# RMS statistics in the MLP phases: eight TensorE sums replaced by a VectorE reduction and two TensorE sums

## The chip, the cores and the metric

The kernel runs on all 8 cores of one Trainium2 chip (trn2). Each core does one half of one sequence, with no communication. The time of an execution is the device time of the slowest core, in microseconds (us). The kernel before takes 1516.05 us in the median of its first three runs (1514.5, 1516.05 and 1701.93). The run of 1701.93 us is counted as slow, a state that some executions had: the cores of one die (cores 0 to 3 or 4 to 7) show a lower granted clock and take longer.

## The reference, cut to what matters

A two-layer backbone block over 4096 tokens of 1024 channels. Every sub-layer starts with an RMS norm, and so does the output:

```python
def rmsnorm(x, g):
    xf = x.astype(jnp.float32)
    y = xf * lax.rsqrt(jnp.mean(xf * xf, axis=-1, keepdims=True) + EPS)
    return (y * g.astype(jnp.float32)).astype(x.dtype)

def sq_relu_mlp(h, w1, w2):
    return jnp.square(jax.nn.relu(h @ w1)) @ w2
# per layer: x = x + g1 * mixer(modulate(rmsnorm(x))); x = x + g2 * sq_relu_mlp(modulate(rmsnorm(x)))
```

The mean of squares over the 1024 channels of each token is the "statistic" of this document.

## The kernel before

Channels lie on the 128 partitions in eight chunks, tokens along the free dimension. A statistic over N tokens therefore sums over eight chunks and over partitions. ScalarE writes the squares as bf16 `[128, 8, N]`; TensorE multiplies each chunk by a matrix of ones/1024 and sums all eight in one bank of PSUM (here the program's `ps`, eight banks of 512 f32 columns, where its matmuls write), which gives the mean on every partition at once:

```python
def norm_sq(tile, sq, part=0, parts=1):          # ScalarE: squares, in `parts` pieces
    c0, c1 = part * NCH // parts, (part + 1) * NCH // parts
    ...
        P.act(sq[:, c0:c1, o:o + n], xv[:, c0:c1, :], AF.Square)

def norm_stat(sq, N, rs):                        # TensorE: eight matmuls of N columns
    bk = P.bank()
    for c in range(NCH):
        P.mm(bk[:, 0:N], ONESM, sq[:, c, 0:N], start=(c == 0), stop=(c == NCH - 1))
    rms_of(bk, N, rs)                            # ScalarE: Ln, Exp -> 1/rms
```

These pieces are issued among the matmuls of the MLP before, one piece per output group, so that the next norm is done when it is needed. `mlp_1` is the up-projection (eight matmuls per output group, then ScalarE's relu from PSUM into one of two buffers `TMP`, then VectorE's square into the hidden tile); `mlp_2` is the down-projection.

```python
nB = sum([st_norm(gb, i) for i in range(3)], [])
spread(mlp_2(ga), nB, 0)                                         # statistics 1, 2, 3
n4, n0 = l1_norm(4, RS[0]), l1_norm(0, RS[1])                    # 4, 5: issued during mlp_2(gb)
...
spread(mlp_2(l1[0]), st_norm(l1[1], 0) + st_norm(l1[1], 1))      # 6, 7
spread(mlp_1(l1[1]), fin_pieces(0) + fin_pieces(1), 2, 2)        # 8, 9: final norm, first two tiles
```

The order of instructions on each engine isn't written by hand. A list scheduler simulates the engines with a cost per instruction, and fixes the order in which each engine will run its instructions.

```python
def ew_cost(self, eng, kind, out, ins):          # the scheduler's idea of a VectorE duration, in ns
    ...
    if sb and (kind == "one" or b16):
        return 155.0 + 0.6 * n
    return 160.0 + 1.04 * n

def pick(e):                                     # the next instruction of engine e
    lim = head[e] + self.WINDOW[e]
    ...                                          # among those within the window: the one that can start
                                                 # first by the simulated times, older ones preferred
```

On the chip each engine gets its list in that order.

The softmax here doesn't subtract the row's maximum and nothing guards it: scores larger than these inputs give would overflow.

Of the kernel before, what the change touches and what calls it, by code (L numbers as in the profile page):

```python
# [7 lines left out]
BF16 = mybir.dt.bfloat16  # L8
AF = mybir.ActivationFunctionType
ALU = mybir.AluOpType  # L10
# [3 lines left out]
NCH = 8  # L14
# [12 lines left out]


class _Op:
    __slots__ = ("id", "eng", "chan", "fn", "deps", "signal", "waits", "pos", "inc", "sigval", "cost", "mode", "unit", "prio")  # L30


class Sched:
# [7 lines left out]
    def __init__(self, nc):  # L41
        self.nc = nc
        self.ops = []
        self.streams = {k: [] for k in ("pe", "act", "dve", "pool", "sp")}
        self.chan_ops = {}
        self.buckets = {}
        self.base = {}
        self.hold, self.boost = None, 0

    def rects(self, ap):  # L50
        name = ap.tensor.name
# [63 lines left out]

    def op(self, eng, fn, reads=(), writes=(), chan=None, inc=1, extra_deps=(), cost=100.0, mode=None, join=False):
        o = _Op()
        o.cost, o.mode, o.prio = cost, mode, self.boost
        if self.hold is not None and eng == "pe":
            join = self.hold > 0  # L120
            self.hold += 1
        o.unit = join
        o.id = len(self.ops)
        o.eng = eng
        o.chan = chan or eng
        o.fn = fn
        o.inc = inc
        o.signal = chan is not None
        o.waits = []
        o.sigval = 0  # L130
        accs = []
        for ap in reads:
            if ap is None or isinstance(ap, (int, float)):
                continue
            sp, rs = self.rects(ap)
            for r in rs:
                accs.append((sp, r, sp == "ps"))
        for ap in writes:
            sp, rs = self.rects(ap)
            for r in rs:  # L140
                accs.append((sp, r, True))
        o.deps = self._query_insert(o, accs)
        for d in extra_deps:
            o.deps[d.id] = True
        self.ops.append(o)
        self.streams[eng].append(o)
        lst = self.chan_ops.setdefault(o.chan, [])
        lst.append(o)
        o.pos = len(lst)
        return o  # L150
# [22 lines left out]
    def reorder(self):  # L173
        ops = self.ops
        units = {e: [] for e in self.streams}
# [18 lines left out]
        head = {e: 0 for e in units}  # L194
# [3 lines left out]
        dma_free, mode = 0.0, None  # L198
# [11 lines left out]
            return v  # L210

        def pick(e):
            lim = head[e] + self.WINDOW[e]
            cand = []
            for i, v in avail[e].items():
                if i < lim:
                    s = max(free[e], v)
                    if e == "pe" and mode is not None and units[e][i][0].mode != mode:
                        s += 100.0
                    cand.append((s, i))  # L220
            if not cand:
                return None
            lo, li = min(cand)
            tol = lo + min(1500.0, max(150.0, 0.5 * sum(o.cost for o in units[e][li])))
            s, i = min(((s, i) for s, i in cand if s <= tol), key=lambda c: c[1] - units[e][c[1]][0].prio)
            return (s, i)
# [5 lines left out]
        while left:  # L232
            e, b = None, None
            for k in units:
                if best[k] is None and avail[k]:
                    best[k] = pick(k)
                if best[k] is not None and (b is None or best[k][0] < b[0]):
                    e, b = k, best[k]
            s, i = b
            t = s  # L240
            for o in units[e][i]:
                for d in o.deps:
                    if unit_of[d] != (e, i):
                        t = max(t, end[d] + (0.0 if ops[d].chan == e == "pe" else self.SEM))
# [8 lines left out]
            if e == "pe":  # L253
                mode = units[e][i][-1].mode
# [80 lines left out]
class Prog:  # L335
# [87 lines left out]
    def stt(self, out, in0, scalar, in1, op0, op1):  # L423
        return self.S.op("dve", lambda e: e.scalar_tensor_tensor(out, in0, scalar, in1, op0, op1),  # L424
                         reads=[in0, in1, scalar], writes=[out], cost=self.ew_cost("dve", "stt", out, [in0, in1]))

    def shuf(self, out, in_, mask):
        return self.S.op("dve", lambda e: e.stream_shuffle(out, in_, mask), reads=[in_], writes=[out],  # L428
                         cost=190.0 + 1.05 * self.n_of(out))
# [61 lines left out]
def build():  # L491
    nc = bass.Bass("TRN2", target_bir_lowering=False)
    P = Prog(nc)
# [27 lines left out]
    def const(name, shape, dt):  # L521
        off = co[0]
        co[0] += (int(np.prod(shape)) * ESZ[dt] + 31) // 32 * 32
        assert co[0] <= 6144, (name, co[0])
        return P.t(name, off, shape, dt)
# [9 lines left out]
    ONESM = const("onesm", [128], BF16)  # L535
# [5 lines left out]
    IDENT = const("ident", [128], F32)  # L541
    MSK = const("msk", [2, 128], BF16)
    EDGE = const("edge", [8, 8], F32)

    XM = P.t("xm", 6144, [NCH, NM], F32)
    E0 = 71680
# [3 lines left out]
    def ft(name, off, shape, dt):  # L550
        return P.t(name, F0 + off, shape, dt)
# [10 lines left out]
    RSALL = ft("rs", 105472, [1216], F32)  # L562
    RS = [RSALL[:, i * 512:(i + 1) * 512] for i in range(2)]
    TMP = [ft("tmp", 110336 + i * 2048, [512], F32) for i in range(2)]


    MBS = [P.bk(7), P.bk(6)]
# [84 lines left out]
    tiles = [[(XM[:, :, t * 512:(t + 1) * 512], 512, 0)] for t in range(4)]  # L652
# [6 lines left out]
    def sqv(buf, N):  # L659
        return buf[:, 0:NCH * N].rearrange("p (a b) -> p a b", a=NCH)  # L660

    def norm_sq(tile, sq, part=0, parts=1):
        c0, c1 = part * NCH // parts, (part + 1) * NCH // parts
        o = 0
        for xv, n, _ in tile:
            P.act(sq[:, c0:c1, o:o + n], xv[:, c0:c1, :], AF.Square)
            o += n
# [2 lines left out]
        P.act(rs[:, 0:N], bk[:, 0:N], AF.Ln, bias=EPSV)  # L670
        P.act(rs[:, 0:N], rs[:, 0:N], AF.Exp, scale=-0.5)

    def norm_stat(sq, N, rs):
        bk = P.bank()
        for c in range(NCH):
            P.mm(bk[:, 0:N], ONESM, sq[:, c, 0:N], start=(c == 0), stop=(c == NCH - 1))
        rms_of(bk, N, rs)

    def norm_apply(tile, rs, l, n, h, c, eng="act", tmps=None):
# [9 lines left out]
                P.ts(h[:, c, o:o + N], tmp, a, b, ALU.mult, ALU.add, eng=eng)  # L689
            o += N  # L690

    def norm_pieces(tile, h, rs, l, n, eng="act", parts=1, tmps=None):

        N = width(tile)
        return [(lambda i=i: norm_sq(tile, h, i, parts)) for i in range(parts)] + [lambda: norm_stat(h, N, rs)] + \
               [(lambda c=c: norm_apply(tile, rs, l, n, h, c, eng, tmps)) for c in range(NCH)]


# [285 lines left out]
    def mlp_2(st):  # L984
        l, g = st["l"], st["g"]
        for fo in range(NCH):
            bks = [P.bank() for _ in st["pieces"]]
            for hf in range(2):
                w = w_take(("w2", l, g, 2 * fo + hf)).rearrange("p (a b) -> p a b", a=16)
                for ti, tile in enumerate(st["pieces"]):  # L990
                    N = width(tile)
                    bk = bks[ti]
                    for h in range(16):
                        P.mm(bk[:, 0:N], w[:, h, :], st["HID"](ti, 16 * hf + h), start=(hf == 0 and h == 0), stop=(hf == 1 and h == 15))
                    if hf == 1:
                        o = 0
                        for xv, n, col in tile:
                            P.stt(xv[:, fo, :], bk[:, o:o + n], MOD[:, l, 40 + fo, col:col + 1], xv[:, fo, :], ALU.mult, ALU.add)
                            o += n
                    if ti == len(st["pieces"]) - 1:  # L1000
                        ST.free()
                    yield 16 * N * MMN

    def spread(main, side, start=0, every=1):

        side = list(side)
        for i, _ in enumerate(main):
            if i >= start and (i - start) % every == 0 and side:
                side.pop(0)()
        for f in side:  # L1010
            f()
# [15 lines left out]
            st["tmp"] = [ft("tmp", 69120 + i * 1664, [416], F32) for i in range(2)]  # L1027
        return st

    def st_norm(st, ti, eng="act", parts=2):  # L1030
        return norm_pieces(st["pieces"][ti], st["H2"][ti], st["rs"][ti], st["l"], 1, eng, parts, st.get("tmp"))

    ga = l0_state(0, [tiles[4], cols(0, 416), cols(416, 416)])
    gb = l0_state(1, [cols(832, 408), cols(1240, 404), cols(1644, 404)])
# [5 lines left out]
    interleave(out_mm(3), nA[2][2:3] + aA[4:] + aB)  # L1040
    ST.fetch(5)
    run_all(mlp_1(ga))
    nB = sum([st_norm(gb, i) for i in range(3)], [])
    spread(mlp_2(ga), nB, 0)
    run_all(mlp_1(gb))

# [16 lines left out]
    HH = {4: sqv(ft("h", 47104, [NCH * 384], BF16), 384), 0: sqv(HB[0], 512), 1: sqv(HB[1], 512), 2: sqv(HB[0], 512), 3: sqv(HB[1], 512)}  # L1063
# [4 lines left out]
    def wo_c(c):  # L1068
        return WO0 if c == 0 else WO17[:, c - 1, :]

    def l1_norm(t, rs, eng="act", parts=2):
        return norm_pieces(tiles[t], HH[t], rs, 1, 0, eng, parts)

    wq, rope_slots, rope_of = [], [], {}

# [138 lines left out]
            yield 4 * 512 * MMN  # L1214


    n4, n0 = l1_norm(4, RS[0]), l1_norm(0, RS[1])

    def early_dma():
        P.dma("pool", WKV0.rearrange("p a b c -> p (a b c)"), d_wkv, slot="wkv")  # L1220
# [60 lines left out]
    l1 = []  # L1281
# [84 lines left out]
    def fin_pieces(t):  # L1366
        xv = tiles[t][0][0]
        rs = RS[t % 2]

        def fin(c):  # L1370
            P.stt(xv[:, c, :], xv[:, c, :], GVEC[:, 4, c:c + 1], rs, ALU.mult, ALU.mult)
            if c % 2 == 1:
                outs.append(P.dma("sp", d_out[:, c - 1:c + 1, t * 512:(t + 1) * 512], xv[:, c - 1:c + 1, :]))
        return [(lambda i=i: norm_sq(tiles[t], sqv(SQF, 512), i, 4)) for i in range(4)] + \
               [lambda: norm_stat(sqv(SQF, 512), 512, rs)] + [(lambda c=c: fin(c)) for c in range(NCH)]

    run_all(mlp_a)
    spread(mlp_2(l1[0]), st_norm(l1[1], 0) + st_norm(l1[1], 1))
    spread(mlp_1(l1[1]), fin_pieces(0) + fin_pieces(1), 2, 2)
    run_all(mlp_2(l1[1]))  # L1380
    for t in (2, 3):
# [121 lines left out]
```

## Time and profile before

| | before |
|---|---|
| time, median of 3 runs | 1516.05 us |
| TensorE (PE) busy | 1431.5 us, 95% |
| VectorE (DVE) / ScalarE (ACT) / GpSimd (POOL) busy | 40% / 39% / 20% |
| share of the chain that ended last | PE 90% |

The page's first part (busy time of each engine, share of the span, instructions) and its fourth (the chain of work that ended last, by engine) for the kernel before:

```profile
PE 1431.5 (95%) x8436; PEld 694.0 (46%) x8436; DVE 600.9 (40%) x1003; ACT 583.2 (39%) x841; POOL 304.5 (20%) x371
PE 90%; DMA 3%; DVE 2%; issue 2%; ACT 1%; POOL 1%; SPq 0%; DVEq 0%; ACTq 0%; POOLq 0%
```

The table by stretches for the kernel before, in the stretches that hold statistics 1, 5, 6, 8 and 9. The columns are the stretch, its length, then busy us and instruction count of PE, PEld, DVE, ACT and POOL, the granted TensorE clock (1.00 is full), the DMA share and GB/s:

```profile
350.00:400.00 50.00, 50.00 (x316) 27.82 (x315) 12.30 (x25) 18.57 (x24) 4.75 (x9) 1.00 0.59 104
650.00:700.00 50.00, 50.00 (x331) 28.25 (x329) 7.07 (x17) 10.21 (x15) 7.05 (x13) 1.00 0.60 105
1150.00:1200.00 50.00, 50.00 (x233) 22.63 (x232) 12.48 (x18) 18.56 (x20) 3.70 (x7) 1.00 0.44 74
1250.00:1300.00 50.00, 50.00 (x234) 22.66 (x232) 16.21 (x24) 15.06 (x22) 3.70 (x7) 1.00 0.45 77
1300.00:1350.00 50.00, 50.00 (x233) 22.64 (x232) 25.97 (x39) 18.14 (x31) 3.70 (x7) 1.00 0.63 124
```

TensorE has no gap in any of them and runs at full clock. The timeline of TensorE before, at the eighth statistic (start, duration, engine, line, operation, output and inputs, count):

```profile
1287.85 1.89 PE L387 MATMUL ps<-h_135,ring_57 128*128 128x512 bf16 x8
1289.58 1.89 PE L387 MATMUL ps<-sqf_176,onesm_46 128*128 128x512 bf16 x8
1291.31 1.89 PE L387 MATMUL ps<-h_136,ring_57 128*128 128x512 bf16 x8
```

From start to start, eight matmuls of 512 columns take 1291.31 - 1289.58 = 1.73 us (216 ns each), whether they do useful products or only sum squares. The printed 1.89 us includes the end of the last, which overlaps the next.

### The profile page before, as it was taken

The page shows a single profiled execution, that of the slowest core. Times are in us where ns is not written, and L with a number is a line of the kernel's source. Part 1 is how long each engine was busy: PE and PEld are TensorE (multiplying, and loading weights), DVE is VectorE, ACT ScalarE, POOL GpSimd, SP SyncE. Part 2 cuts the span into 40 slices and gives each one's busy share as a digit, 9 for nine tenths or more (in the row PEclk, how much of TensorE's full clock was granted, in tenths as well). Part 3 has the DMA queues.
Part 4 walks back from the last instruction along what each step waited for, and adds up shares of the span by engine and source line. Part 5 has one row for each costly group of instructions (what it writes and reads, how often), then busy time and mean ns, then how long its engine had stood idle before and what let it go on. Part 6 is the DMA issues. An engine that isn't in the chain of part 4 may idle for free.

```text
span 1514.3 us, 23295 instructions; the slowest of 8 cores (1505.0 to 1514.3 us)
## 1 busy us (share of the span) xinstructions
PE 1431.5 (95%) x8436; PEld 694.0 (46%) x8436; DVE 600.9 (40%) x1003; ACT 583.2 (39%) x841; POOL 304.5 (20%) x371
## 2 busy tenths in 40 slices
PE   1699999999999999999997999899999999999996
PEld 0344445555555555555543334334444444444442
DVE  0177874443221344322248666443443222552003
ACT  2464363335110333323018778774334121432002
POOL 2025400010100010110135666552000000000000
PEclk9999999999999999999998999999999999999998
DMA  9554715545663455664354000400444444663432
GB/s 193 152 126 70 131 28 94 98 84 90 118 113 63 77 89 104 104 108 74 62 94 74 8 2 2 70 2 15 72 82 70 80 74 71 134 130 70 84 56 111
DMA packets 39808, 124.16 MB, mean 82 GB/s; under 512 B 4240, under 2 KB 4624, under 8 KB 39312
## 3 DMA queue, kind: packets, MB, share of 16 engines
q0 software_dynamic: 29504, 102.90, 39.9%
q1 hardware_dynamic: 10192, 19.76, 4.1%
q8 instruction: 70, 1.15, 0.3%
q14 instruction: 42, 0.34, 0.1%
HBM read 217.15 MB, written 8.39 MB: 149 GB/s over the span
## 4 chain that ended last, share of the span: by engine, by line
PE 90%; DMA 3%; DVE 2%; issue 2%; ACT 1%; POOL 1%; SPq 0%; DVEq 0%; ACTq 0%; POOLq 0%
PE ps L387 89%; DMA xm_55<-xT 2%; DMA ring_59<-ada_r 1%; DVE xm_55 L424 0%; SPq L447 0%; DVE tmp_65 L414 0%; ACT xb_68 L397 0%; POOL qt_122 L414 0%; ACT rs_63 L397 0%; DVE tb_129 L414 0%; DVE tb_130 L428 0%; DVE tb_127 L414 0%; POOL dt_75 L414 0%; DVE tb_128 L414 0%; DVE tb_130 L414 0%
## 5 line engine op out<-in xcount | busy, mean ns | idle before, releaser
L424 DVE SCALAR_TENSOR_TENSOR xm_55<-ps,mod_44,xm_55 128x512 f32<-128x512 f32 (+2 forms) x136 | 97.4, 718 | 296.4 <-PE ps L387 296.1
L397 ACT ACTIVATE tmp_64<-ps 128x512 f32<-128x512 f32 (+2 forms) x156 | 84.8, 543 | 213.6 <-PE ps L387 161.8
L397 ACT ACTIVATE tmp_65<-ps 128x512 f32<-128x512 f32 (+2 forms) x157 | 85.3, 544 | 159.5 <-PE ps L387 98.1
L397 ACT ACTIVATE sqf_176<-xm_55 128x1024 bf16<-128x1024 f32 x16 | 16.7, 1053 | 158.9 <-DVE xm_55 L424 156.9
L387 PE MATMUL ps<-xb_68,win_67 128*128 128x512 bf16 (+1 forms) x192 | 50.2, 422 | 10.2 <-ACT xb_68 L397 9.5
L387 PE MATMUL ps<-h_0_98,ring_61 128*128 128x408 bf16 (+3 forms) x336 | 58.9, 335 | 0.0
L387 PE MATMUL ps<-h_0_98,ring_58 128*128 128x384 bf16 (+3 forms) x336 | 58.9, 335 | 0.0
L414 DVE TENSOR_TENSOR tmp_64<-xm_55,rs_63 128x512 f32<-128x512 f32 (+2 forms) x44 | 33.8, 767 | 48.2 <-ACT rs_63 L397 41.9
L397 ACT ACTIVATE rs_63<-ps,epsv_51 128x512 f32<-128x512 f32 (+3 forms) x16 | 10.6, 666 | 105.2 <-PE ps L387 104.9
L387 PE MATMUL ps<-hid_99,ring_61 128*128 128x416 bf16 (+3 forms) x288 | 51.0, 335 | 0.0
L387 PE MATMUL ps<-h_0_98,ring_60 128*128 128x416 bf16 (+3 forms) x288 | 50.5, 335 | 0.0
L387 PE MATMUL ps<-h_0_98,ring_57 128*128 128x416 bf16 (+3 forms) x288 | 50.4, 335 | 0.0
L387 PE MATMUL ps<-h_0_98,ring_59 128*128 128x416 bf16 (+3 forms) x288 | 50.4, 335 | 0.0
L447 POOL DMA_DIRECT2D ring_59<-w_r x27 | 14.3, 531 | 171.8 <-PE ps L387 171.7
L414 DVE TENSOR_TENSOR hid_100<-tmp_64 128x416 bf16<-128x416 f32 (+3 forms) x48 | 27.9, 581 | 43.8 <-ACT tmp_64 L397 43.8
L414 DVE TENSOR_TENSOR hid_99<-tmp_64 128x416 bf16<-128x416 f32 (+3 forms) x48 | 27.9, 581 | 41.2 <-ACT tmp_64 L397 41.1
L387 PEld LDWEIGHTS ps<-h_0_98,ring_61 128*128 128x128 bf16 x336 | 32.5, 97 | 25.1 <-issue 0.6
L387 PEld LDWEIGHTS ps<-h_0_98,ring_58 128*128 128x128 bf16 x336 | 32.4, 98 | 25.0 <-issue 0.8
L447 POOL DMA_DIRECT2D ring_61<-w_r x27 | 14.3, 530 | 143.3 <-PE ps L387 143.1
L414 DVE TENSOR_TENSOR hid_99<-tmp_65 128x416 bf16<-128x416 f32 (+3 forms) x48 | 27.9, 581 | 37.7 <-ACT tmp_65 L397 37.7
L414 DVE TENSOR_TENSOR hid_100<-tmp_65 128x416 bf16<-128x416 f32 (+3 forms) x48 | 27.9, 581 | 36.0 <-ACT tmp_65 L397 36.0
L447 POOL DMA_DIRECT2D ring_60<-w_r x24 | 12.7, 530 | 138.4 <-PE ps L387 103.7
(803 smaller groups left out, 3136.9 us busy)
## 6 DMA issues: line engine op xcount, KB each, us to landing
ring_61<-w_r POOLq DMA_DIRECT2D x27, 512.0 KB, 5.7
ring_59<-w_r POOLq DMA_DIRECT2D x27, 512.0 KB, 5.8
ring_58<-w_r POOLq DMA_DIRECT2D x26, 512.0 KB, 5.8
ring_57<-w_r POOLq DMA_DIRECT2D x24, 512.0 KB, 5.8
ring_60<-w_r POOLq DMA_DIRECT2D x24, 512.0 KB, 5.9
outT<-xm_55 SPq DMA_DIRECT2D x16, 512.0 KB, 4.9
xm_55<-xT SPq DMA_DIRECT2D x6, 1024.0 KB, 9.0
ring_58<-ada_r POOLq DMA_DIRECT2D x12, 512.0 KB, 5.2
```

The source lines that it names most:

```text
L387: return self.S.op("pe", lambda e: e.matmul(out, lhsT, rhs, start=start, stop=stop), reads=[lhsT, rhs], writes=[out], cost=max(30.0 if hal ...
L397: return self.S.op("act", lambda e: e.activation(out, in_, func, bias=bias, scale=scale), reads=[in_, scale, bias], writes=[out], cost=175 ...
L414: return self.S.op(eng, lambda e: e.tensor_tensor(out, in0, in1, op), reads=[in0, in1], writes=[out], cost=self.ew_cost(eng, "tt", out, [i ...
L424: return self.S.op("dve", lambda e: e.scalar_tensor_tensor(out, in0, scalar, in1, op0, op1), reads=[in0, in1, scalar], writes=[out], cost= ...
L447: return self.S.op(q, lambda e: e.dma_start(out=out, in_=in_), reads=[in_], writes=[out], chan="dma:" + slot, inc=16, extra_deps=dep, cost ...
```

## The change

The sum over the eight chunks moves to VectorE, which has time; only one vector of sums per partition is left for TensorE. That vector is f32, and to keep its precision in bf16 matmuls it is split in two bf16 parts (the rounded value and the rest), so two matmuls remain of eight. Only the nine statistics listed above are changed. The core of the diff:

```diff
+    def addc(self, out, in_):
+
+        return self.S.op("dve", lambda e: e.tensor_reduce(out, in_.rearrange("p c n -> p n c"), mybir.AxisListType.X, ALU.add),
+                         reads=[in_], writes=[out], cost=160.0 + 1.04 * self.n_of(in_))
...
+    SQHI = const("sqhi", [512], BF16)
...
     TMP = [ft("tmp", 110336 + i * 2048, [512], F32) for i in range(2)]
+    SQLO = ft("sqlo", 110336 + 2048, [512], BF16)
...
-    def norm_stat(sq, N, rs):
+    def norm_stat(sq, N, rs, red=False):
         bk = P.bank()
-        for c in range(NCH):
-            P.mm(bk[:, 0:N], ONESM, sq[:, c, 0:N], start=(c == 0), stop=(c == NCH - 1))
+        if red:
+            P.addc(TMP[0][:, 0:N], sq[:, :, 0:N])
+            P.copy(SQHI[:, 0:N], TMP[0][:, 0:N])
+            P.tt(SQLO[:, 0:N], TMP[0][:, 0:N], SQHI[:, 0:N], ALU.subtract)
+            P.mm(bk[:, 0:N], ONESM, SQHI[:, 0:N], start=True, stop=False)
+            P.mm(bk[:, 0:N], ONESM, SQLO[:, 0:N], start=False, stop=True)
+        else:
+            for c in range(NCH):
+                P.mm(bk[:, 0:N], ONESM, sq[:, c, 0:N], start=(c == 0), stop=(c == NCH - 1))
         rms_of(bk, N, rs)
...
-    nB = sum([st_norm(gb, i) for i in range(3)], [])
+    nB = sum([st_norm(gb, i, red=True) for i in range(3)], [])
...
-    n4, n0 = l1_norm(4, RS[0]), l1_norm(0, RS[1])
+    n4, n0 = l1_norm(4, RS[0], red=True), l1_norm(0, RS[1], red=True)
...
-               [lambda: norm_stat(sqv(SQF, 512), 512, rs)] + [(lambda c=c: fin(c)) for c in range(NCH)]
+               [lambda: norm_stat(sqv(SQF, 512), 512, rs, t < 2)] + [(lambda c=c: fin(c)) for c in range(NCH)]
...
-    spread(mlp_2(l1[0]), st_norm(l1[1], 0) + st_norm(l1[1], 1))
+    spread(mlp_2(l1[0]), st_norm(l1[1], 0, red=True) + st_norm(l1[1], 1, red=True))
```

(The diff also adds a field `pin` to the scheduler, which nothing sets; it changes no order. The rest passes `red` through.) The reduction reads its input as `p n c`: for each token the eight values lie N bf16 values apart.

More of the change, by code (lines that the diff above doesn't have):

```diff
@@ L29 @@
 class _Op:
-    __slots__ = ("id", "eng", "chan", "fn", "deps", "signal", "waits", "pos", "inc", "sigval", "cost", "mode", "unit", "prio")
+    __slots__ = ("id", "eng", "chan", "fn", "deps", "signal", "waits", "pos", "inc", "sigval", "cost", "mode", "unit", "prio", "pin")
 class Sched:
@@ L47, in __init__ @@
         self.base = {}
-        self.hold, self.boost = None, 0
+        self.hold, self.boost, self.pin = None, 0, False
     def rects(self, ap):
@@ L117, in op @@
         o = _Op()
-        o.cost, o.mode, o.prio = cost, mode, self.boost
+        o.cost, o.mode, o.prio, o.pin = cost, mode, self.boost, self.pin and eng == "pe"
         if self.hold is not None and eng == "pe":
@@ L212, in pick @@
         def pick(e):
-            lim = head[e] + self.WINDOW[e]
+            lim = head[e] + (1 if head[e] < len(units[e]) and units[e][head[e]][0].pin else self.WINDOW[e])
             cand = []
@@ L690, in norm_apply, with norm_pieces @@
             o += N
-    def norm_pieces(tile, h, rs, l, n, eng="act", parts=1, tmps=None):
+    def norm_pieces(tile, h, rs, l, n, eng="act", parts=1, tmps=None, red=False):
         N = width(tile)
-        return [(lambda i=i: norm_sq(tile, h, i, parts)) for i in range(parts)] + [lambda: norm_stat(h, N, rs)] + \
+        return [(lambda i=i: norm_sq(tile, h, i, parts)) for i in range(parts)] + [lambda: norm_stat(h, N, rs, red)] + \
                [(lambda c=c: norm_apply(tile, rs, l, n, h, c, eng, tmps)) for c in range(NCH)]
@@ L1028, in l0_state, with st_norm @@
         return st
-    def st_norm(st, ti, eng="act", parts=2):
-        return norm_pieces(st["pieces"][ti], st["H2"][ti], st["rs"][ti], st["l"], 1, eng, parts, st.get("tmp"))
+    def st_norm(st, ti, eng="act", parts=2, red=False):
+        return norm_pieces(st["pieces"][ti], st["H2"][ti], st["rs"][ti], st["l"], 1, eng, parts, st.get("tmp"), red)
     ga = l0_state(0, [tiles[4], cols(0, 416), cols(416, 416)])
@@ L1069, in wo_c, with l1_norm @@
         return WO0 if c == 0 else WO17[:, c - 1, :]
-    def l1_norm(t, rs, eng="act", parts=2):
-        return norm_pieces(tiles[t], HH[t], rs, 1, 0, eng, parts)
+    def l1_norm(t, rs, eng="act", parts=2, red=False):
+        return norm_pieces(tiles[t], HH[t], rs, 1, 0, eng, parts, red=red)
     wq, rope_slots, rope_of = [], [], {}
```

## The prediction

> **What bounds the kernel now.** TensorE. The page gives PE 1431.5 us of 1514.3 us (95%); the chain that ended last is 90% PE. In a table by 50 us stretches, PE is busy 50.0 us at a granted clock of 1.00 in every stretch from 200 to 750 us and from 1050 to 1450 us. All nine changed statistics lie there: three in the first layer's MLP down-projection (at 365, 398, 431 us), two in the next one (641, 697), two in the third (1167, 1207), two under the last up-projection (1290, 1336). A TensorE microsecond saved there is a microsecond of the kernel. VectorE (40%) has room.
>
> **Removed.** Of eight matmuls against the ones matrix, two remain. Spacing of starts in the timeline: 216 ns at 512 columns, 171 ns at 404, about 163 ns at 384. Five statistics have 512 columns, three 404 to 408, one 384: 6 x (5 x 0.216 + 3 x 0.171 + 0.163) = 10.5 us, 0.7%.
>
> **Added.** On VectorE, per statistic: a reduction over 8 x N bf16 values, a copy to bf16, a subtraction. No reduction is in the trace. [...]the trace's [...]operation (128x512 f32 product, 0.69 us) gives about 1.04 ns per element plus 0.16 us, so I estimate 4.4 us for 512 columns, 3.5 for 404, 3.4 for 384; copy about 0.45, subtraction 0.58 to 0.69 us. Together about 45 us more VectorE time, off the critical path.
>
> **Moved.** In the instruction order the pairs stand on TensorE exactly where the eight stood, except the last two, which come four output groups (6.9 us) later. The attention stage is unchanged on every engine.
>
> **Does TensorE wait for the chain?** From the end of the last square to the old statistic's start the trace has 6.1 us (first), 6.0 (fourth), 7.2 (fifth), 7.0 us (sixth); the chain needs about 4.7, 4.5, 5.7, 5.8 us. So slack is about 1.3 us each. The second, third and seventh are loose; the two last have about 7 us against 5.7. I expect no wait. In the last two, VectorE's 5.7 us delay the squaring of hidden units: some four PSUM banks of backlog out of eight, which should not stop TensorE.
>
> **The doubt.** The reduction reads with a stride of N, never two neighbours. [...]At 1.73 the 512 reduction takes 7.2 us and six of the nine pairs would hold TensorE 0.7 to 1.5 us each, 6.5 us in all, leaving 4 us of gain. I give this one in three.
>
> **Prediction.** 1516 - 10.5 = 1505.5 us with a full-rate reduction, 1512 with a slow one; I put it at 1507.0 us, range 1502.0 to 1513.0. Faster by over 2%: 0.01; within 2%: 0.98; slower by over 2%: 0.01.
>
> **What would show it.**
> - Right: nine reductions of 3.4 to 4.5 us; PE instructions down by 54, PE busy by about 10 us; VectorE busy up by about 45 us; no TensorE idle time before the pairs.
> - Half right: reductions of about 7 us, and TensorE idle 0.7 to 1.5 us before a pair.
> - Wrong: PE idle in the last up-projection released by ScalarE (no free bank), or a longer attention stage.
>
> **What would make it wrong.** A reduction slower still (each further us costs up to 6 us); backlog under the last up-projection; an attention stage that shifts when it starts at another phase against its weight loads; run-to-run spread.

The sum came to 1516 - 10.5 = 1505.5 us with a full-rate reduction and to 1516 - 10.5 + 6.5 = 1512 us with a slow one, and was put at 1507.0 us. The full rate is an estimate: products in the trace of the kernel before take 692 ns at 512 columns and 558 ns at 384, about 1.04 ns per element plus 0.16 us, and that is taken over for a reduction, of which that trace has none. The slow rate, 1.73 (ns per element), was not measured when it was put on record; the changed kernel then showed (7202 - 160) / 4096 = 1.72 ns.

## The result, and the profile after

The changed kernel took 1519.63 us in the median of 4 runs (1518.56 to 1522.2), all fast. The ratio to the kernel before is 1.0031, with a 95% interval of 1.0007 to 1.0055. Ratios here are the mean time of one kernel's fast runs over that of the other's fast runs of the same rounds, so they aren't quite the ratio of the medians. This first one rests on two fast runs of the kernel before and four of the changed one. The change did not gain 9 us; it lost about 0.0031 x 1516 = 4.7 us.

The page of the changed kernel, the same two lines:

```profile
PE 1419.9 (94%) x8297; PEld 689.0 (45%) x8382; DVE 667.9 (44%) x1030; ACT 581.2 (38%) x841; POOL 303.8 (20%) x371
PE 85%; DVE 6%; DMA 3%; issue 2%; ACT 2%; POOL 1%; SPq 0%; DVEq 0%; ACTq 0%; POOLq 0%
```

TensorE's busy time fell by 11.6 us (some matmul records are missing here, so the count of weight loads, PEld, is the better one: 8436 - 8382 = 54, as the diff says). But VectorE is now 6% of the chain that ended last, and its busy time rose by 67 us, not by 45. The groups of VectorE instructions of the changed kernel say why (line, engine, operation, output and input with shapes, count; then busy us and mean ns of one; then the idle time before and what ended it):

```profile
L429 DVE TENSOR_REDUCE tmp_65<-h_137 128x512 f32<-128x4096 bf16 x2 | 14.4, 7202 | 3.9 <-PE ps L387 2.7 <-ACT h_137 L397 1.2
L429 DVE TENSOR_REDUCE tmp_65<-sqf_178 128x512 f32<-128x4096 bf16 x2 | 14.2, 7109 | 0.2
L429 DVE TENSOR_REDUCE tmp_65<-h_0_100 128x404 f32<-128x3232 bf16 x2 | 11.3, 5667 | 0.0
L429 DVE TENSOR_REDUCE tmp_65<-h_139 128x384 f32<-128x3072 bf16 x1 | 5.4, 5440 | 1.2 <-ACT h_139 L397 1.2
```

A reduction at 512 columns takes 7.1 to 7.2 us, not 4.4. The same five stretches of the changed kernel (this page's slowest core is core 4, the one before was core 1; stretches are read by themselves):

```profile
350.00:400.00 50.00, 49.33 (x316) 26.98 (x315) 26.23 (x33) 19.77 (x25) 5.02 (x10) 1.00 0.57 100
650.00:700.00 50.00, 46.70 (x296) 26.37 (x296) 14.36 (x16) 7.69 (x9) 4.93 (x10) 0.97 0.65 111
1150.00:1200.00 50.00, 48.40 (x221) 21.86 (x225) 29.07 (x25) 17.92 (x19) 3.58 (x7) 1.00 0.47 74
1250.00:1300.00 50.00, 46.86 (x208) 20.88 (x212) 19.53 (x19) 10.55 (x17) 3.17 (x6) 0.97 0.47 74
1300.00:1350.00 50.00, 46.84 (x209) 20.90 (x212) 31.52 (x38) 19.50 (x32) 3.70 (x7) 0.98 0.63 116
```

TensorE now has gaps, and in three of the five the granted clock is below 1. The waits of TensorE that are new (who waited for whom: us in total, times, longest):

```profile
PE ps L387 <- DVE sqhi_55 L442: 6.4, 4, 2.6
PE ps L387 <- DVE sqlo_67 L414: 4.9, 6, 3.2
```

That is 11.3 us of waiting before the pairs on this core, more than the 10.5 us saved. The timeline of the changed kernel at the eighth statistic shows one such wait whole (some lines left out):

```profile
1289.24 7.10 DVE L429 TENSOR_REDUCE tmp_65<-sqf_178 128x512 f32<-128x4096 bf16 x1
...
1292.55 1.89 PE L387 MATMUL ps<-h_137,ring_59 128*128 128x512 bf16 x7
1296.43 1.06 ACT L397 ACTIVATE sqf_178<-xm_56 128x1024 bf16<-128x1024 f32 x1 [8.09 <-DVE tmp_65 L429]
1296.44 0.43 DVE L442 CAST sqhi_55<-tmp_65 128x512 bf16<-128x512 f32 x1
1296.97 0.69 DVE L414 TENSOR_TENSOR sqlo_67<-tmp_65,sqhi_55 128x512 bf16<-128x512 f32 x1
1297.01 0.47 PE L387 MATMUL ps<-sqhi_55,onesm_46 128*128 128x512 bf16 x1 [2.57 <-DVE sqhi_55 L442]
1297.81 0.58 PE L387 MATMUL ps<-sqlo_67,onesm_46 128*128 128x512 bf16 x1 [0.32 <-DVE sqlo_67 L414]
...
1298.19 3.07 PE L387 MATMUL ps<-h_138,ring_59 128*128 128x512 bf16 x8
1301.10 1.24 PE L387 MATMUL ps<-h_137,ring_60 128*128 128x512 bf16 x5
```

TensorE ends its group at 1294.4 us and stands until 1297.0, when the first part of the sum is there. Then something second happens: the next eight matmuls need 1301.10 - 1298.19 = 2.91 us instead of 1.73. The table by stretches of 3 us around the same place shows the granted clock fall:

```profile
1292.00:1295.00 3.00, 2.39 (x11) 0.89 (x10) 3.00 (x1) 0.00 (x0) 0.00 (x0) 1.00 0.75 147
1295.00:1298.00 3.00, 0.66 (x2) 0.23 (x3) 2.46 (x3) 1.06 (x1) 0.00 (x0) 0.86 0.00 0
1298.00:1301.00 3.00, 3.00 (x9) 1.08 (x8) 1.66 (x3) 2.77 (x5) 0.00 (x0) 0.57 0.01 3
1301.00:1304.00 3.00, 3.00 (x16) 1.37 (x14) 2.34 (x4) 1.40 (x3) 0.53 (x1) 1.00 0.34 41
```

(1 - 0.86) x 3 + (1 - 0.57) x 3 = 1.7 us of full-speed time are lost, so the clock was at half for about 3.4 us (read in steps of 0.5 us, it is 0.50 in every step from 1297.5 to 1300.5 us). I read the wait and the clock after each pair in the same way on all eight cores of the changed kernel:

| statistic | 1 | 2, 3, 7 | 4 | 5 | 6 | 8 | 9 |
|---|---|---|---|---|---|---|---|
| wait before the pair, us, mean of 8 cores | 0.67 | 0 | 0.23 | 2.9 | 1.3 | 2.9 | 3.0 |
| cores whose clock then fell to half | 0 | 0 | 0 | 4 | 0 | 8 | 7 |

The waits sum to 11.0 us, the clock to 19 x 1.7 / 8 = 4.0 us per core. So -10.5 + 11.0 + 4.0 = +4.5 us, against 4.7 measured. That the two are so close is partly luck: the measured interval goes from 1 to 8 us. And the clock also falls to half in the attention stage (about 780 to 1050 us), in both kernels and by core: added up as above, the loss there is 5.1 to 11.9 us per core in either profile, 8.3 us in the mean of the cores before and 6.4 after.

That stage also shows that the length of a wait alone does not decide whether the clock falls. In the profile of the kernel before, at about 850 us, TensorE of every core has a wait of 1.3 us and soon after one of 0.5; on cores 1, 4, 5 and 6 the clock then fell to half, on the other four it did not. What decides is not shown here.

### The profile page after: what moved, and what is told of

Read it like the earlier page. It is cut to its first block, busy times and chain, and to the rows that moved or that the text cites. A ratio compares the mean times of both kernels' runs of the same rounds, so it can differ in the third digit from the quotient of the medians.

```text
span 1517.9 us, 23136 instructions; the slowest of 8 cores (1510.5 to 1517.9 us)
## 1 busy us (share of the span) xinstructions
PE 1419.9 (94%) x8297; PEld 689.0 (45%) x8382; DVE 667.9 (44%) x1030; ACT 581.2 (38%) x841; POOL 303.8 (20%) x371
## 4 chain that ended last, share of the span: by engine, by line
PE 85%; DVE 6%; DMA 3%; issue 2%; ACT 2%; POOL 1%; SPq 0%; DVEq 0%; ACTq 0%; POOLq 0%
PE ps L387 85%; DVE tmp_65 L429 3%; DMA xm_56<-xT 2%; DMA ring_59<-ada_r 1%; ACT rs_64 L397 0%; DVE xm_56 L424 0%; SPq L452 0%; DVE tmp_66 L414 0%; ACT xb_70 L397 0%; POOL qt_124 L414 0%; DVE tb_129 L414 0%; DVE tb_131 L414 0%; DVE sqlo_67 L414 0%; DVE tmp_65 L414 0%; DVE tb_132 L433 0%
## 5 line engine op out<-in xcount | busy, mean ns | idle before, releaser
L387 PE MATMUL ps<-xb_70,win_69 128*128 128x512 bf16 (+1 forms) x190 | 49.7, 420 | 10.3 <-ACT xb_70 L397 9.5
L387 PE MATMUL ps<-h_0_100,ring_62 128*128 128x408 bf16 (+3 forms) x336 | 58.9, 334 | 0.0
L387 PE MATMUL ps<-h_0_100,ring_59 128*128 128x384 bf16 (+3 forms) x336 | 58.9, 335 | 0.0
L387 PE MATMUL ps<-hid_101,ring_62 128*128 128x416 bf16 (+3 forms) x288 | 51.0, 335 | 0.0
L387 PE MATMUL ps<-h_0_100,ring_61 128*128 128x416 bf16 (+3 forms) x288 | 50.5, 335 | 0.0
L387 PE MATMUL ps<-h_0_100,ring_60 128*128 128x416 bf16 (+3 forms) x288 | 50.4, 335 | 0.0
L387 PE MATMUL ps<-h_0_100,ring_58 128*128 128x416 bf16 (+3 forms) x288 | 50.4, 335 | 0.0
L414 DVE TENSOR_TENSOR tmp_65<-xm_56,rs_64 128x512 f32<-128x512 f32 (+2 forms) x44 | 33.2, 754 | 34.2 <-ACT rs_64 L397 27.9
L414 DVE TENSOR_TENSOR hid_102<-tmp_65 128x416 bf16<-128x416 f32 (+3 forms) x48 | 27.9, 581 | 43.5 <-ACT tmp_65 L397 43.5
L414 DVE TENSOR_TENSOR hid_101<-tmp_65 128x416 bf16<-128x416 f32 (+3 forms) x48 | 27.9, 581 | 41.6 <-ACT tmp_65 L397 41.5
L414 DVE TENSOR_TENSOR hid_101<-tmp_66 128x416 bf16<-128x416 f32 (+3 forms) x48 | 27.9, 581 | 37.3 <-ACT tmp_66 L397 37.3
L387 PEld LDWEIGHTS ps<-h_0_100,ring_62 128*128 128x128 bf16 x336 | 32.5, 97 | 25.1 <-issue 0.6
L414 DVE TENSOR_TENSOR hid_102<-tmp_66 128x416 bf16<-128x416 f32 (+3 forms) x48 | 27.9, 581 | 36.4 <-ACT tmp_66 L397 36.4
L387 PEld LDWEIGHTS ps<-h_0_100,ring_59 128*128 128x128 bf16 x336 | 32.4, 98 | 25.0 <-issue 0.8
```

What stands on the lines that cost most here:

```text
L387: return self.S.op("pe", lambda e: e.matmul(out, lhsT, rhs, start=start, stop=stop), reads=[lhsT, rhs], writes=[out], cost=max(30.0 if hal ...
L414: return self.S.op(eng, lambda e: e.tensor_tensor(out, in0, in1, op), reads=[in0, in1], writes=[out], cost=self.ew_cost(eng, "tt", out, [i ...
```

## The experiments

Theory 1: the saving is real and critical; it is taken back because the reduction is slower than its cost in the scheduler, so that the pairs stand too early in TensorE's list; the longer waits also cost clock. Rivals are named with each run. Each run is compared with runs of the kernel before on the same chip.

| run | what | median us | ratio to before (95%) |
|---|---|---|---|
| e1_two_of_eight | savings without costs (wrong result) | 1506.92 | 0.9927 (0.9915 to 0.9940) |
| e2_cost_told | scheduler told the measured cost | 1507.24 | 0.9931 (0.9919 to 0.9943) |
| e3_neighbours | reduction over neighbours (wrong result) | 1508.93 | 0.9938 (0.9924 to 0.9952) |
| e4_loose_only | statistics 2, 3, 7 only | 1514.52 | 0.9979 (0.9966 to 0.9992) |
| e5_last_two | 8, 9 only | 1525.12 | 1.0052 (1.0039 to 1.0065) |
| e6_last_two_one_later | 8, 9 only, pairs 1.7 us later | 1519.17 | 1.0008 (0.9994 to 1.0022) |
| e7_first_seven | 1 to 7 only | 1516.79 | 0.9996 (0.9982 to 1.0009) |
| e8_tree | additions instead of the reduction | 1506.33 | 0.9922 (0.9907 to 0.9937) |
| e9_step_4_bytes | one look (wrong result) | 1506.7 | - |
| e10_step_32_bytes | one look (wrong result) | 1522.55 | - |
| e11_tree_three_more | additions, three more statistics | 1500.43 | 0.9899 (0.9881 to 0.9917) |

Medians are over all runs, a few slow ones included. The medians of the kernel before were 1518.01 us beside e1 to e4, 1517.51 beside e5 to e8 and 1514.76 beside e9 to e11.

### Is the saving real? (e1_two_of_eight)

```diff
         if red:
-            P.addc(...); P.copy(...); P.tt(...); P.mm(... SQHI ...); P.mm(... SQLO ...)
+            for c in range(2):
+                P.mm(bk[:, 0:N], ONESM, sq[:, c, 0:N], start=(c == 0), stop=(c == 1))
```

> Wrong result on purpose: the nine statistics sum only two of the eight chunks, with two matmuls and nothing on VectorE. It holds what the change removes and nothing of what it adds. Theory 1 (the 54 matmuls are worth their 10.5 us, and TensorE's waits for the slow reduction took it back): 10.5 us faster than before, ratio 0.993. Rival (the matmuls saved are not on the critical path, or another limit takes the time back): ratio 0.997 to 1.000.

Measured: 0.9927, that is 11 us (9 to 13), with a wrong result as intended. The 54 matmuls are worth what was computed for them; the rival falls. The costs are in what was added.

### Is it only the place of the pairs? (e2_cost_told)

```diff
-                         reads=[in_], writes=[out], cost=160.0 + 1.04 * self.n_of(in_))
+                         reads=[in_], writes=[out], cost=160.0 + 1.74 * self.n_of(in_))
```

> The changed kernel with one number different: the scheduler's cost of the reduction is 1.74 instead of 1.04 ns per element, as the trace measured it. The same instructions run; the pairs of the six tight statistics come 16 matmuls (2.7 to 3.5 us) later on TensorE. Theory 1 (the pairs stood too early for the real reduction): TensorE's 11.3 us of waiting before the pairs falls under 2 us, ratio to before 0.993 to 0.995. Rival A (VectorE's 8 us stretch itself stops TensorE, through PSUM banks not emptied in the last up-projection): waits for ScalarE or VectorE appear there in place of the waits at the pairs, ratio about 0.998 to 1.000. Rival B (the chain of dependent steps costs the same wherever it stands): ratio stays near 1.003.

Measured: correct, 0.9931. The reductions are as slow as before, and yet the whole saving is there. From the groups of VectorE instructions and from the waits of TensorE of this run:

```profile
L429 DVE TENSOR_REDUCE tmp<-sqf 128x512 f32<-128x4096 bf16 x2 | 14.4, 7206 | 0.2
PE ps L387 <- DVE sqlo L414: 0.5, 1, 0.5
```

One wait of 0.5 us is all that is left of 11.3 on the slowest core. The six tight pairs stand 16 matmuls later in TensorE's list, and some VectorE instructions of the norms move with them. Rival A falls with it: VectorE is held for more than 8 us in the last up-projection here too (7.21 + 0.42 + 0.69 = 8.3 us), and TensorE has no gap for want of a PSUM bank: from 1270 to 1310 us it was busy for 40.00 us on six of the eight cores and for 39.79 and 39.84 us on the other two (some matmul records are missing there), and the waits of the slowest core list none for the instructions that empty a bank there (`tmp`, `hid`). Rival B (a chain costs the same wherever it stands) falls as well.

### Why is the reduction slow? (e3_neighbours, e9_step_4_bytes, e10_step_32_bytes)

```diff
-    e.tensor_reduce(out, in_.rearrange("p c n -> p n c"), ...)
# e3: eight neighbouring values (step 2 bytes)
+    e.tensor_reduce(out, in_.rearrange("p c n -> p (c n)").rearrange("p (n c) -> p n c", c=NCH), ...)
# e9 (t = 2, step 4 bytes) and e10 (t = 16, step 32 bytes; t = 4, step 8 bytes, at 404 and 408 columns)
+    e.tensor_reduce(out.rearrange("p (m t) -> p m t", t=t),
+                    in_.rearrange("p c n -> p (c n)").rearrange("p (m c t) -> p m t c", c=NCH, t=t), ...)
```

All three sum the wrong values; the number of elements, types and buffers stay as in the changed kernel, and so did TensorE's order of instructions.

> Wrong result on purpose: the reduction adds eight neighbouring values (step 1) instead of eight values N apart; count, type, buffers, orders on all engines stay as in the changed kernel. Theory 1 (each element in another place is what makes it slow): 4.4 us instead of 7.2 us at 512 columns, TensorE's waits before the pairs fall from 11.3 to about 1 us, ratio 0.993 to 0.995. Rival (a reduction with a 4-byte output is slow whatever it reads): still 7.2 us, ratio 1.003.

> Wrong result on purpose: the reduction adds eight values two apart (4 bytes), so that one value after another comes from the neighbouring 4-byte word and never two from one word; all else as in the changed kernel. If what matters is the distance of the jump (a near word costs nothing): 4.4 us at 512 columns as in the run with neighbouring values. If what matters is that no two values in succession share a word: 7.2 us as in the changed kernel.

> Wrong result on purpose: as the run before, with steps of 16 values (32 bytes) at 512 and 384 columns and of 4 values (8 bytes) at 404 and 408. Distance of the jump decides: between 4.4 and 7.2 us, or 4.4. Any jump costs alike: 7.2 us at 512, 5.4 at 384 and 5.7 at 404 columns.

Groups of VectorE instructions in the run with neighbours:

```profile
L429 DVE TENSOR_REDUCE tmp<-h 128x512 f32<-128x4096 bf16 x3 | 13.3, 4420 | 4.2 <-PE ps L387 2.7 <-ACT h L397 1.5
```

The same with steps of 4 bytes, in the run e9:

```profile
L429 DVE TENSOR_REDUCE tmp<-h 128x512 f32<-128x4096 bf16 x3 | 13.3, 4420 | 4.2 <-PE ps L387 2.7 <-ACT h L397 1.6
```

The same with steps of 32 bytes (first line) and of 8 bytes (second line), in the run e10:

```profile
L429 DVE TENSOR_REDUCE tmp<-h 128x512 f32<-128x4096 bf16 x3 | 22.7, 7558 | 4.2 <-PE ps L387 2.7 <-ACT h L397 1.5
L429 DVE TENSOR_REDUCE tmp<-h 128x404 f32<-128x3232 bf16 x2 | 7.0, 3509 | 0.0
```

With neighbours the reduction takes 4.42 us, exactly the estimate of 1.04 ns per element plus 0.16 us, TensorE waits 1.2 us in all before the pairs, and the ratio is 0.9938: theory 1 holds, and the rival that a reduction with this output is always slow falls. With steps of 4 bytes it is 4.42 us as well, with 8 bytes still at full rate (3.51 us at 404 columns, as with neighbours), with 32 bytes 7.56 us, slower even than the changed kernel's jump of 1024 bytes (7.2 us). So the distance decides, and the border lies between 8 and 32 bytes; my two guesses for e9 are thereby decided for the first. A step of 16 bytes wasn't tried, and why the border lies there is not shown. e9 and e10 were run once each: what they show is the duration of the reductions, not a time of the kernel.

### Does the slow reduction hurt where nothing waits for it? (e4_loose_only)

```diff
-    nB = sum([st_norm(gb, i, red=True) for i in range(3)], [])
+    nB = sum([st_norm(gb, i, red=i > 0) for i in range(3)], [])
# and red=True only for st_norm(l1[1], 1); eight matmuls for n4, n0, st_norm(l1[1], 0) and the final norm
```

> Only the second, third and seventh statistic are reduced on VectorE, those with over 20 us between squares and sums; six stay on eight matmuls. The reductions are as slow as in the changed kernel but nothing waits for them. Theory 1: 6 x (2 x 0.171 + 0.216) = 3.3 us faster than before, ratio 0.9978, no wait before the pairs. Rival (a long VectorE reduction hurts wherever it stands): ratio 1.000 or above.

Measured: 0.9979, that is 3.2 us, all that the matmuls are worth (3.3 us); these three pairs have no wait in the table of the changed kernel either. The slow reduction was harmless where the list leaves it time.

### Where was the loss? (e5_last_two, e7_first_seven)

```diff
# e5: red only in fin_pieces (t < 2)         e7: red everywhere but there
-   norm_stat(sqv(SQF, 512), 512, rs, t < 2)
+   norm_stat(sqv(SQF, 512), 512, rs)          # e7
```

> Only the eighth and ninth statistic (under the last up-projection) are reduced on VectorE; seven stay on eight matmuls. Theory 1 with the clock (a wait of about 2.9 us before a pair also drops the granted clock to about half for some 3.4 us, a loss of 1.7 us each): 2.6 us saved, 5.8 us waited, 3.4 us lost in clock, 6.6 us slower than before, ratio 1.0043. Without the clock term: 3.2 us slower, ratio 1.002. Rival (the loss arises in the down-projections): ratio 0.998.

> The complement: the seven statistics in the down-projections are reduced on VectorE, the last two stay on eight matmuls. Theory 1: 7.9 us saved, about 5.5 us waited (3.2 of it before the fifth pair), 1.7 us lost in clock after the fifth: 0.7 us faster than before, ratio 0.9995; the loss against the saving is mostly in the last two. Rival (the loss is spread evenly over the nine): ratio about 1.0024.

Measured: 1.0052 for the last two alone, 0.9996 for the other seven alone. The two under the last up-projection lose about 8 us; the seven in the down-projections just pay for themselves. In e7 the clock fell to half after the fifth pair on six of the eight cores. TensorE's waits in e5:

```profile
PE ps L387 <- DVE sqhi L442: 5.2, 2, 2.6
PE ps L387 <- DVE sqlo L414: 0.8, 2, 0.4
```

6.0 us for two pairs, close to the 5.8 expected. The clock term needs care. In this run the halved clock was seen after only 5 of 16 such waits, fewer than the 15 of 16 in the changed kernel; but cores 0 to 3, all of one die, were held at 0.81 from about 1310 us on, some ten us after the first wait, and their mean clock from 1310 to 1370 us is 0.95, about 3 us lost. In the mean of the eight cores the halved clock lost 1.3 us (one of the five stretches lasted twice as long as the others) and the 0.81 about 1.5, so -2.6 + 6.0 + 2.8 = +6.2 us against 8 measured (6 to 10): the size is explained roughly, not exactly, and the clock did not fall as Theory 1 said, after both waits on every core.

### Is it the length of the wait? (e6_last_two_one_later)

```diff
 # e5, and:
-                         reads=[in_], writes=[out], cost=160.0 + 1.04 * self.n_of(in_))
+                         reads=[in_], writes=[out], cost=160.0 + 1.3 * self.n_of(in_))
```

> As the run before, but with the reduction's cost at 1.3 ns per element in the scheduler, which puts each of the two pairs one output group (8 matmuls, 1.7 us) later on TensorE. Theory 1 with a clock that falls only after the longer waits: the wait falls from 2.9 to about 1.2 us each, no drop of the granted clock, so 3.4 us less waiting and 3.4 us less clock loss than in the run before: about equal to the kernel before, ratio 0.9995 to 1.0005. If each us of waiting costs clock in proportion: clock still lost, ratio about 1.001.

```profile
PE ps L387 <- DVE sqhi L442: 1.8, 2, 1.0
PE ps L387 <- DVE sqlo L414: 0.8, 2, 0.4
```

These are the waits of TensorE in that run. With each pair one output group of eight matmuls later, the waiting falls from 6.0 to 2.6 us and the time by 0.0044 x 1516 = 6.7 us: 3.4 us of waiting and about as much again, of which the clock accounts for some 2 us (2.8 us lost per core in e5's profile, 0.7 in this one). No core had a halved clock after a wait in this run (waits of 1.26 to 1.38 us, 16 in all). The ratio, 1.0008, lies a little above the range that I gave (0.9995 to 1.0005). Cores 2 and 3 again were at 0.81 for some microseconds after the first pair (0.96 in the mean from 1310 to 1370 us); that, like what sets off the halving, isn't explained here.

### Versions for use (e8_tree, e11_tree_three_more)

If the jump is the trouble, add whole rows: chunk on chunk, so that both inputs are read along the tokens. In bf16, in place, in the squares' own buffer; the last sum goes to TensorE as it is, so one matmul is left and no `TMP` buffer is held.

```diff
         if red:
-            ...                                   # reduction, copy, subtraction, two matmuls
+            for k in (4, 2, 1):
+                P.tt(sq[:, 0:k, 0:N], sq[:, 0:k, 0:N], sq[:, k:2 * k, 0:N], ALU.add)
+            P.mm(bk[:, 0:N], ONESM, sq[:, 0, 0:N], start=True, stop=True)
# e11 only:
-    nA = [st_norm(ga, i) for i in range(3)]
+    nA = [st_norm(ga, i, red=True) for i in range(3)]
```

> A version for use: instead of the reduction, three bf16 additions in place (4N, 2N, N values, each of neighbouring values), and one matmul instead of a pair. Theory 1: the additions take about 1.2, 0.7 and 0.4 us at 512 columns (a third of the reduction), no wait before the sums, 63 matmuls saved: 6 x 10.5 / 6 x 7 / 6 = 12.3 us faster than before, ratio 0.992; error within what the reference check allows. Rival (VectorE work in these phases costs TensorE something whatever its length): ratio 0.995 or above.

> The version with additions, extended to the three statistics of the first MLP (at about 190 to 210 us of the kernel before, 416, 416 and 384 columns), which the change left on eight matmuls. Saved on TensorE in addition: 7 x (2 x 0.176 + 0.163) = 3.6 us, if TensorE is the limit there as its full busy share says: ratio 0.9898. If VectorE, 80% busy until shortly before, holds the pairs there: ratio 0.992, like the version without.

Groups of VectorE instructions in e8:

```profile
L414 DVE TENSOR_TENSOR h<-h 128x2048 bf16<-128x2048 bf16 x3 | 3.7, 1226 | 2.9 <-ACT h L397 2.9
L414 DVE TENSOR_TENSOR h<-h 128x1024 bf16<-128x1024 bf16 x3 | 2.1, 692 | 0.3
L414 DVE TENSOR_TENSOR h<-h 128x512 bf16<-128x512 bf16 x3 | 1.3, 425 | 0.3
```

The three additions take 1.226 + 0.692 + 0.425 = 2.34 us, a third of the one reduction (from 1024 to 2048 values the time grows by 0.53 us, 0.52 ns per value, half of the 1.04), and their costs in the scheduler are close (155 ns plus 0.6 ns per value). In e8 no wait before a sum is left. In e11 one is: on the slowest core TensorE waits 1.7 us, once, for the additions of an MLP statistic (`PE ps L387 <- DVE h L414: 1.7, 1, 1.7`). Both results pass the comparison with the reference, although the sums are rounded to bf16. Measured: 0.9922 and 0.9899, against 0.992 and 0.9898 expected. Both versions beat the kernel before and the changed kernel; e11, at 1500.43 us, is the fastest, though its interval (0.9881 to 0.9917) overlaps that of e8 (0.9907 to 0.9937), so what the three added statistics gain is not shown by itself.

## Why the prediction was wrong, point by point

- **TensorE bounds the MLP phases, and 54 matmuls are worth 10.5 us: right.** e1 measured 11 us (9 to 13), e2 got 10.5.
- **"I estimate 4.4 us for 512 columns": this step failed.** It measured 7.2 us. The prediction had named the doubt and its size (1.73 ns per element, 7.2 us), and gave it one in three; it was the case (1.72 ns measured). e3 and e9 show the estimate to be right for a reduction over near values, e10 and the changed kernel that it doesn't hold for jumps of 32 bytes (7.56 us) and 1024 bytes (7.2 us).
- **"At 1.73 [...] 6.5 us in all, leaving 4 us of gain": this step failed too, and it is why even the slow branch, 1512 us, was missed.** Two terms were mis-sized.
  - The waits were 11.0 us instead of 6.5. The prediction gave only the range, 0.7 to 1.5 us each; worked out from its slacks and chains, with 0.69 ns more per element, the four tight down-projection pairs (1, 4, 5 and 6) come to about 0.9, 0.6, 1.3 and 1.6 us. Three stayed below that (0.67, 0.23, 1.3), the fifth took 2.9. There the reduction did not start with the end of the squares (681.23 + 3.70 = 684.93 us) but 2 us later. It writes into `TMP[0]`, and by the kernel's allocation that memory also holds, in the same phase, squares of another statistic (`SQP`, at the same address), which TensorE had not yet summed. The trace of the changed kernel, in the order of time:

```profile
681.23 3.70 ACT L397 ACTIVATE h_137<-xm_56 128x2048 bf16<-128x2048 f32 x2
686.51 0.38 PE L387 MATMUL ps<-sqp_143,onesm_46 128*128 128x512 bf16 x1
687.00 7.13 DVE L429 TENSOR_REDUCE tmp_65<-h_137 128x512 f32<-128x4096 bf16 x1 [2.69 <-PE ps L387]
...
695.60 0.38 PE L387 MATMUL ps<-sqlo_67,onesm_46 128*128 128x512 bf16 x1 [3.25 <-DVE sqlo_67 L414]
```

  - For the last two I said "about 7 us against 5.7" from a count of groups; in the trace TensorE reaches the pair 5.2 us after the reduction starts (1289.24 to 1294.4). So they waited 2.9 to 3.0 us, not 1.5 at most.
  - The clock was not in the sum at all. After waits of 2.7 to 3.3 us before a pair the granted clock fell to half in 19 of 24 cases, 1.7 us each, 4.0 us per core (in e5 in 5 of 16, in e7 in 6 of 8). After waits up to 1.4 us before a pair it never did (none of 24 in the changed kernel, none of 16 in e6); in the attention stage it fell after waits of 1.3 and 0.5 us on four of eight cores. Where the long waits are missing, no such fall was seen: in the profile of the kernel before, the granted clock was 1.00 on all eight cores from 200 to 750 and from 1050 to 1450 us, in that of e2 it was 1.00 on all eight from 1270 to 1370 us. At the eighth statistic the wait was not one gap but two with one matmul between them (2.57 and 0.32 us), and these already cost.
- **"VectorE's 5.7 us delay the squaring [...] should not stop TensorE": right**, even at 8.3 us: in e2 TensorE shows no wait for a bank there.
- **"The attention stage is unchanged": right.** PE busy in the stretch from 800 to 1040 us was 223.8 us before and 221.4 after, and its longest waits (4.9 and 4.8 us for ScalarE, 2.4 and 2.4 for VectorE) are the same ones. (The trace of the changed kernel lacks some matmul records there.)
- **Chances:** within 2% was right; 1519.63 us lies above the stated range. The range took "slow" as the worst case and did not ask what a wait costs besides its length.

## What to carry to other kernels

Moving work from the limiting engine to an idle one gains only if the limiting engine never reaches the result early: look up the slack at each place, and where a static order is made from a cost model, measure the new instruction first and correct its cost (here one number, 1.04 to 1.74, turned +0.3% into -0.7%). A reduction over a far stride can be slow: at steps of 1024 bytes it took 7.2 us, at 2 and 4 bytes 4.42 us, and adding whole rows, at 2.34 us, was three times faster than the first on this shape. And a gap in TensorE can cost more than its length, when the clock falls behind it: in this kernel a wait of about 3 us then cost 4.7. It fell after 19 of 24 such waits in the changed kernel and after 5 of 16 in e5, so count with this cost as a risk.
